# First layer of a two-layer decoder step: the row sums of the mixing weights, from four TensorE products with ones to one GpSimd sum over the partitions

## The chip, the cores and the metric

One core of a Trainium2 chip runs the whole step as one program. The metric is the device time of one execution in microseconds, the median over several runs. Beside it stands one execution that the hardware profiler recorded; its times count from its first instruction. The engines are TensorE (PE in the profile; its weight loads are PEld), VectorE (DVE), ScalarE (ACT), GpSimd (POOL) and SyncE (SP), which here issues all transfers.

## The reference

One inference step over 256 new prompt tokens and 8 x 8 sample tokens, all in float32. Layer 0 mixes tokens with a chunked spatial gating, layer 1 with a matrix memory; each layer ends with a gated MLP with a short convolution. The change touches only the mixer of layer 0:

```python
h = jax.nn.gelu(x @ w_in)
u, v = jnp.split(h, 2, axis=-1)
mu = jnp.mean(v, -1); var = jnp.mean(jnp.square(v - mu), -1)
v = (v - mu) * lax.rsqrt(var + EPS) * ln_g + ln_b
ws = jnp.where(mask, w_s[:, :L, :L], 0.0)          # 8 groups, L = 128
mixed = jnp.einsum('gts,bnsgd->bntgd', ws, vc) + b_s[:, :L].T[:, :, None]
y = (u * mixed.reshape(bsz, s, D_A)) @ w_out
```

`ln_b` is the same for every token s, so its part of the mixture is `ln_b` times the sum of `ws` over s. The kernel uses that: it mixes the normalised values without gain and shift, multiplies by the gain afterwards, and adds `ln_b` times these row sums. The row sums, one number for each of 8 groups and 128 target tokens, are what the change computes in another way.

## The kernel before

**Precision.** Weights and activations are float32. TensorE multiplies rounded halves: each operand is split into a rounded high half and the rest (`wh`, `wl` for weights, `xh`, `xl` for activations), and three products, high by high, high by low and low by high, are added in PSUM. For each chunk of weights, a tile of 128 partitions by up to 1024 elements, ScalarE casts the high half (L177) and VectorE subtracts it from the raw tile to get the low half (L178). The raw tiles have four buffers, the halves three; a buffer is taken again when TensorE has used the chunk three places before it.

**The order of the work in layer 0.** First come the values v, in natural layout (tokens on partitions), in four groups of 512 columns (`group(0)` to `group(3)`, products into `pv_a`); each group takes four chunks of 1024 columns. Between them lie the first norm (`rc`, made by GpSimd in L296), its spread over the partitions (`pb`), and, in `load_ws`, the transfers of the mixing weights `ws`, of a triangular mask `trit`, of the sample weights `wss` with their mask `bdt`, and of the biases `bs`. GpSimd then multiplies `ws` by the mask (L408) and both quarters of `wss` by theirs (L410). `v_out(q)` takes a group out of PSUM: gelu on ScalarE (L440), the joining of the sample parts (L435, L436) and statistics (L441).

After that come 16 blocks for u (`pm`, 24 products of 320 columns each). Behind block 0 stand `row_sums` and `v_stats`. `row_sums` splits the masked `ws` into two halves (`wsh` on ScalarE, `wsl` on VectorE, both L358), multiplies a matrix of ones by them (`pr`, two products for each half of the columns, so that every partition of the result holds the sums), and ScalarE copies the result into `rsum` (named `rs_a` in the profile, L421). `v_stats` joins the statistics and has GpSimd take the reciprocal root `rs` (`rstd_a`, L476); `normalise` (L482, ScalarE) applies it to the values. `mix(b)`, from block 4 on, multiplies the values by `ws` and `wss` (`pmix`), makes `b2` from `rsum`, `ln_b` and the biases (L519, VectorE), and then y (L522, L525, L528), which is split for the output projection.

**What sets the order.** TensorE's instructions, and most transfers, run in the order in which the program is written (`pin`). On ScalarE, VectorE and GpSimd a planner of the kernel language places each instruction in its engine's queue by modelled costs and by what it depends on; `issue_after` keeps an instruction behind another one. On the chip each engine then runs its queue in that fixed order, and waits where a semaphore has not been reached. The masking products L408 and L410 stand behind `rc`; the split of `ws` stands behind the latest weight split (`behind_split`).

Of the kernel before, what the change touches and what calls it, by code (L numbers as in the profile page):

```python
# [9 lines left out]

F32 = mybir.dt.float32
F32R = mybir.dt.float32r
# [4 lines left out]
P = 128  # L17
# [8 lines left out]
NH = 8  # L26
# [12 lines left out]
def halves(t):  # L39

    return t.rearrange("p (a b) -> p a b", a=2)


def parity(x):

    return x.rearrange("p (b a) -> p a b", a=2)
# [12 lines left out]
class Net:  # L59
# [301 lines left out]
    def layer_a(self):  # L361
        nc, tc, I, O = self.nc, self.tc, self.I, self.O
        with tc.tile_pool(name="ya", bufs=1) as yp, tc.tile_pool(name="la", bufs=1) as lp:
# [8 lines left out]
            ws = lp.tile([P, NH, P], F32, name="ws_a")  # L372
            wss = lp.tile([P, NH, P], F32, name="wss_a")
            bs = lp.tile([P, NH, P], F32, name="bs_a")
            rsum = lp.tile([P, NH, P], F32, name="rs_a")
# [21 lines left out]
            def load_ws():  # L397
# [9 lines left out]
                with tc.issue_after(self.rc_made.ins):  # L407
                    nc.gpsimd.tensor_tensor(ws, ws, trit.unsqueeze(1).to_broadcast([P, NH, P]), op=MULT)  # L408
                    for r, c in quads:
                        nc.gpsimd.tensor_tensor(wss[r, :, c], wss[r, :, c], bdt[r].unsqueeze(1).to_broadcast([64, NH, 64]), op=MULT)  # L410

            def row_sums():
                wsh = lp.tile([P, NH, P], F32R, name="wsh")
                wsl = lp.tile([P, NH, P], F32R, name="wsl")
                with self.behind_split():
                    self.split(wsh, wsl, ws)
                for i in range(2):
                    pr = self.psa.tile([P, 512], F32, tag="pa", name="pr")
                    for w, a, z in ((wsh, True, False), (wsl, False, True)):
                        self.mm(pr, self.onesr, w[:, 4 * i:4 * i + 4, :].rearrange("p g t -> p (g t)"), a, z)  # L420
                    nc.scalar.copy(rsum[:, 4 * i:4 * i + 4, :].rearrange("p g t -> p (g t)"), pr)  # L421

            def group(q, hooks, k=0):
                if q not in vps:
# [45 lines left out]
            def v_stats():  # L470
                for r, o in ((slice(64, P), slice(0, 64)), (slice(0, 64), slice(64, P))):
                    nc.scalar.copy(sts[r, 4:, :], sts[o, :4, :])
                for t in range(3):
                    nc.vector.bn_aggr(mv[:, t, :], st[:, t] if t < 2 else sts)
                nc.vector.tensor_scalar(ve, mv[:, :, 1], EPS, None, op0=ADD)
                nc.gpsimd.tensor_tensor(rs, ve, self.mhalf.to_broadcast([P, 3]), op=ALU.pow)  # L476
                nc.vector.scalar_tensor_tensor(ve, mv[:, :, 0], -1.0, rs, op0=MULT, op1=MULT)

            def normalise(q):
                for t in range(3):  # L480
                    vv = v[:, t, q * 512:(q + 1) * 512] if t < 2 else vs[:, 2 * q:2 * q + 2, :]
                    nc.scalar.activation(vv, vv, AF.Identity, scale=rs[:, t:t + 1], bias=ve[:, t:t + 1])  # L482
# [3 lines left out]
            def gains_in(q):  # L486
                cs = slice(q * 512, (q + 1) * 512)
                gB = lp.tile([P, 512], F32, tag="gB", name="gB", bufs=2)
                bB = lp.tile([P, 512], F32, tag="bB", name="bB", bufs=2)
                for par, r in enumerate((slice(64, P), slice(0, 64))):  # L490
                    self.pin(nc.sync.dma_start(gB[r], I["a_ln_g"][par:par + 1, cs].to_broadcast([64, 512])))
                    self.pin(nc.sync.dma_start(bB[r], I["a_ln_b"][par:par + 1, cs].to_broadcast([64, 512])))
                gains.append((gB, bB))
# [13 lines left out]
            def mix(b):  # L507
                g = b // 2
                pm = self.psa.tile([P, 512], F32, tag="pa", name="pmix")
                for t in range(2):  # L510
                    self.mm(pm[:, t * P:(t + 1) * P], v[:, t, b * P:(b + 1) * P], ws[:, g, :], True, True)
                if b % 2 == 0:

                    self.mm(pm[:, TP:TP + P], vs[:, g, :], wss[:, g, :], True, True)
                    ms[g] = pm[:, TP:TP + 64]
                    ms[g, 1] = pm[:, TP + 64:TP + P]
                sm = ms.pop((g, 1)) if b % 2 else ms.pop(g)
                b2 = lp.tile([P, 1, P], F32, tag="b2", name="b2", bufs=2)
                nc.vector.scalar_tensor_tensor(b2, rsum[:, g:g + 1, :], self.vec(V_LB + b), bs[:, g:g + 1, :], op0=MULT, op1=ADD)  # L519
                y = self.tp.tile([P, T], F32, tag="yf", name="y_a", bufs=2)  # L520
                lg = self.vec(V_LG + b)
                nc.vector.scalar_tensor_tensor(  # L522
                    y[:, :TP].rearrange("p (c t) -> p c t", c=2), pm[:, :TP].rearrange("p (c t) -> p c t", c=2), lg,
                    b2.to_broadcast([P, 2, P]), op0=MULT, op1=ADD)
                nc.vector.scalar_tensor_tensor(  # L525
                    y[:, TP:].rearrange("p (b t) -> p b t", b=NB), sm.rearrange("p (b t) -> p b t", b=NB), lg,
                    b2[:, :, :NS].to_broadcast([P, NB, NS]), op0=MULT, op1=ADD)
                nc.vector.tensor_tensor(y, y, us.pop(b), op=MULT)  # L528
                self.split_y(yh[:, b, :], yl[:, b, :], y)
# [4 lines left out]
            for b in range(16):  # L534
                ps = self.block(KD, self.x_rhs)
                if b == 0:
                    row_sums()
                    v_stats()
                t = lp.tile([P, T], F32, tag="ur", name="ur", bufs=2)
                nc.vector.tensor_tensor(halves(t), parity(ps[:, :T]), halves(self.rb), op=MULT)  # L540
                u = lp.tile([P, T], F32, tag="u", name="u", bufs=6)
                nc.scalar.activation(u, t, AF.Gelu_apprx_tanh)
                us[b] = u
                if 2 <= b < 2 + len(tables):
                    with tc.issue_after(self.last_load.ins):
                        nc.sync.dma_start(*tables[b - 2])
                if b in (9, 12):
                    gains_in(b // 3 - 3)
                if b in (0, 3, 6, 9):
                    normalise(b // 3)  # L550
                while mixed < min(b, b - 4 + max(0, b - 4) // 3 + 1):
                    mix(mixed)
                    mixed += 1
# [855 lines left out]
```

## Time and profile before

| | us |
|---|---|
| median of 3 runs | 882.37 |
| lowest, highest | 881.98, 882.60 |
| span of the profiled execution (first to last instruction) | 880.8 |
| TensorE busy in it | 874.7 (99%) |
| VectorE busy | 670.7 (76%) |
| ScalarE busy | 512.0 (58%) |
| GpSimd busy | 118.5 (13%) |

The profile gives no time of its own for the profiled execution beside the span; the median of the runs lies 1.6 us above it, which is what lies around the first and the last instruction.

A row of the timeline reads: start in us, duration in us (of all instructions merged in the row), engine, line, operation, output tile `<-` inputs, shapes, count, and in brackets the idle time before it with what ended it. A row of the view of one tile reads: line, engine, operation, tile, count, shortest / median / longest duration in ns, first and last start in us, forms. A row of DMA issues ends with the size of one and the us from issue to landing. The mean granted TensorE clock of the run was 0.999 of full speed.

### The profile page before, as it was taken

To read this page: it belongs to the slowest core of one execution; us is meant where nothing else is said; L and a number is where in the kernel's file an instruction comes from. 1 tells how busy PE (TensorE), PEld (TensorE's weight loads), DVE (VectorE), ACT (ScalarE), POOL (GpSimd) and SP (SyncE) were. 2 spreads that over 40 slices of the span, in tenths; PEclk is the share of its full clock that TensorE was granted. 3 is DMA by queue.
4 is the path that set the end of the run, shared out by engine and by line. 5 is a ranking of instruction groups with operands and counts; after the bars stand their busy time and mean duration, and the time that the engine had idled before them with its cause. 6 is when DMAs were issued, how large, how long until landed. Compare 5 with 4: busy or idle time off the path is not lost.

```text
span 880.8 us, 16999 instructions
## 1 busy us (share of the span) xinstructions
PE 874.7 (99%) x6424; PEld 857.2 (97%) x6424; DVE 670.7 (76%) x1291; ACT 512.0 (58%) x930; POOL 118.5 (13%) x288
## 2 busy tenths in 40 slices
PE   9999999999999999999999999999999999999997
PEld 7889999999999999999999999999999999999997
DVE  6866986578878865558999998878988788786443
ACT  6658554465555544347777775656766555554442
POOL 3200000020000000002433222303001000100000
PEclk9999999999999999999999999999999999999999
DMA  8755645545554455554847876665664544555551
GB/s 262 231 181 165 189 146 170 172 155 161 163 168 161 152 164 169 157 170 144 249 142 231 248 222 217 200 210 168 194 224 145 168 156 157 169 161 165 155 151 60
DMA packets 54950, 155.76 MB, mean 177 GB/s; under 512 B 7460, under 2 KB 12716, under 8 KB 54868
## 3 DMA queue, kind: packets, MB, share of 16 engines
q1 hardware_dynamic: 54868, 154.67, 55.9%
q8 instruction: 51, 0.84, 0.4%
q14 instruction: 31, 0.25, 0.1%
HBM read 142.66 MB, written 11.99 MB: 176 GB/s over the span
## 4 chain that ended last, share of the span: by engine, by line
PE 99%; DMA 0%; DVE 0%; ACT 0%; POOL 0%; issue 0%
PE pm L80 84%; PE pv_a L80 6%; PE num L80 2%; PE pmix L80 1%; PE pcs L80 1%; PE psc L80 1%; PE pCp L80 1%; PE phn L83 1%; PE pv L83 1%; PE pc L80 0%; DMA xT<-in_xv 0%; PE pk L83 0%; DVE y_p L687 0%; PE pg L80 0%; PE pb L80 0%; PE pr L80 0%
## 5 line engine op out<-in xcount | busy, mean ns | idle before, releaser
L178 DVE TENSOR_TENSOR wl<-raw,wh 128x1024 fp32r<-128x1024 f32 (+4 forms) x254 | 298.3, 1176 | 115.5 <-ACT wh L177 114.5
L177 ACT CAST wh<-raw 128x1024 fp32r<-128x1024 f32 (+4 forms) x254 | 255.5, 1007 | 215.5 <-PE pm L80 145.0
L80 PE MATMUL pm<-xh,wh 128*128 128x320 f32 x1216 | 356.6, 301 | 0.0
L80 PE MATMUL pm<-xl,wh 128*128 128x320 f32 x1216 | 354.7, 299 | 0.0
L80 PE MATMUL pm<-xh,wl 128*128 128x320 f32 x1216 | 308.9, 299 | 0.0
L80 PEld LDWEIGHTS pm<-xl,wh 128*128 128x128 f32 x1216 | 230.2, 189 | 0.1
L80 PEld LDWEIGHTS pm<-xh,wh 128*128 128x128 f32 x1216 | 230.1, 189 | 0.1
L80 PEld LDWEIGHTS pm<-xh,wl 128*128 128x128 f32 x1216 | 212.1, 189 | 0.0
L80 PE MATMUL pm<-yh_f,wh 128*128 128x320 f32 x352 | 105.3, 299 | 0.0
L80 PE MATMUL pm<-yh_f,wl 128*128 128x320 f32 x352 | 105.3, 299 | 0.0
L80 PE MATMUL pm<-yl_f,wh 128*128 128x320 f32 x352 | 105.3, 299 | 0.0
L80 PEld LDWEIGHTS pm<-yh_f,wl 128*128 128x128 f32 x352 | 66.6, 189 | 0.0
L80 PEld LDWEIGHTS pm<-yl_f,wh 128*128 128x128 f32 x352 | 66.6, 189 | 0.0
L80 PEld LDWEIGHTS pm<-yh_f,wh 128*128 128x128 f32 x352 | 66.6, 189 | 0.0
L593 DVE SCALAR_TENSOR_TENSOR fcv<-fpad,vecs,fcv 128x336 f32<-128x336 f32 x88 | 49.6, 566 | 2.1 <-ACT fcv L591 0.7
L595 ACT ACTIVATE fgl<-fcv 128x256 f32<-128x256 f32 x44 | 18.3, 416 | 37.3 <-DVE fcv L593 37.3
L80 PE MATMUL pm<-yh_a,wh 128*128 128x320 f32 x128 | 38.4, 300 | 0.0
L80 PE MATMUL pm<-yh_a,wl 128*128 128x320 f32 x128 | 38.3, 299 | 0.0
L80 PE MATMUL pm<-yl_a,wh 128*128 128x320 f32 x128 | 38.3, 299 | 0.0
L347 DVE TENSOR_TENSOR xT<-pm,xT 128x320 f32<-128x320 f32 x39 | 19.0, 486 | 24.4 <-PE pm L80 24.4
L80 PE MATMUL pm<-yhb,wh 128*128 128x320 f32 x128 | 35.9, 304 | 0.0
L80 PE MATMUL pm<-ylb,wh 128*128 128x320 f32 x128 | 35.5, 300 | 0.0
(273 smaller groups left out, 1263.8 us busy)
## 6 DMA issues: line engine op xcount, KB each, us to landing
raw<-in_f_up SPq DMA_DIRECT2D x88, 512.0 KB, 3.5
raw<-in_b_win SPq DMA_DIRECT2D x48, 512.0 KB, 4.5
raw<-in_f_dn SPq DMA_DIRECT2D x32, 448.0 KB, 3.3
C<-in_C SPq DMA_DIRECT2D x32, 258.0 KB, 4.9
out_Cs<-C SPq DMA_DIRECT2D x32, 258.0 KB, 4.8
raw<-in_a_win SPq DMA_DIRECT2D x16, 512.0 KB, 3.6
raw<-in_a_wo SPq DMA_DIRECT2D x16, 512.0 KB, 3.7
raw<-in_f_dn SPq DMA_DIRECT2D x16, 512.0 KB, 3.5
```

The lines of the kernel that those rows point to most:

```text
L80: self.pin(self.nc.tensor.matmul(out, lhsT, rhs, start=start, stop=stop, skip_group_check=skip))
L83: self.pin(self.nc.tensor.transpose(out, in_, ident))
L177: self.last_split = self.hold(nc.scalar.copy(wh[:, :kn, :], raw[:, :kn, :]))
L178: self.last_low = nc.vector.tensor_tensor(wl[:, :kn, :], raw[:, :kn, :], wh[:, :kn, :].bitcast(F32), op=SUB)
L347: self.nc.vector.tensor_tensor(x, ps[:, :T], x, op=ADD)
L593: nc.vector.scalar_tensor_tensor(cv, pd[:, i:i + NC], self.vec(w + i * KF), cv, op0=MULT, op1=ADD)
L595: nc.scalar.activation(gl[:, :TP], cv[:, :TP], AF.Gelu_apprx_tanh)
```

## The change

`row_sums` goes, with its call behind block 0: the split of `ws` into `wsh` and `wsl`, four products with ones, two copies out of PSUM. In its place `load_ws` gets one GpSimd instruction behind the masking products, which sums the masked `ws` (128 partitions x 1024 elements) over the partitions in float32 and writes the sums to all 128 partitions of `rsum`. The reader of `rsum`, L519, is unchanged.

```diff
+from concourse.bass_isa import ReduceOp
@@ load_ws, in tc.issue_after(self.rc_made.ins)
                     nc.gpsimd.tensor_tensor(ws, ws, trit.unsqueeze(1).to_broadcast([P, NH, P]), op=MULT)
                     for r, c in quads:
                         nc.gpsimd.tensor_tensor(wss[r, :, c], wss[r, :, c], bdt[r].unsqueeze(1).to_broadcast([64, NH, 64]), op=MULT)
-
-            def row_sums():
-                wsh = lp.tile([P, NH, P], F32R, name="wsh")
-                wsl = lp.tile([P, NH, P], F32R, name="wsl")
-                with self.behind_split():
-                    self.split(wsh, wsl, ws)
-                for i in range(2):
-                    pr = self.psa.tile([P, 512], F32, tag="pa", name="pr")
-                    for w, a, z in ((wsh, True, False), (wsl, False, True)):
-                        self.mm(pr, self.onesr, w[:, 4 * i:4 * i + 4, :].rearrange("p g t -> p (g t)"), a, z)
-                    nc.scalar.copy(rsum[:, 4 * i:4 * i + 4, :].rearrange("p g t -> p (g t)"), pr)
+                    nc.gpsimd.partition_all_reduce(rsum.rearrange("p g t -> p (g t)"), ws.rearrange("p g t -> p (g t)"), P, ReduceOp.add)
@@ the 16 blocks
             for b in range(16):
                 ps = self.block(KD, self.x_rhs)
                 if b == 0:
-                    row_sums()
                     v_stats()
```

## The prediction

> **What bounds the kernel now.** I read the page's busy times and chain first, then what is removed by its tiles, then TensorE in order of time around the four products.
>
> ```profile
> span 880.8 us, 16999 instructions
> PE 874.7 (99%) x6424; PEld 857.2 (97%) x6424; DVE 670.7 (76%) x1291; ACT 512.0 (58%) x930; POOL 118.5 (13%) x288
> PE 99%; DMA 0%; DVE 0%; ACT 0%; POOL 0%; issue 0%
> ```
>
> TensorE is busy for 874.7 of 880.8 us and 99% of the chain that ended last is TensorE's own order. So the time changes only by what is taken out of TensorE's order, or by what makes TensorE wait where it does not wait now. GpSimd is busy 13% and has room.
>
> ```profile
> L358 ACT CAST wsh<-ws_a x1: 1048/1048/1048, 58.9 to 58.9; 128x1024 fp32r<-128x1024 f32 x1
> L358 DVE TENSOR_TENSOR wsl<-ws_a,wsh x1: 1219/1219/1219, 60.2 to 60.2; 128x1024 fp32r<-128x1024 f32 x1
> L421 ACT COPY rs_a<-pr x2: 587/590/592, 66.8 to 67.3; 128x512 f32<-128x512 f32 x2
> ...
> 65.08 0.39 PE L80 MATMUL pr<-wsh,onesr 128*128 128x512 f32 x1
> ...
> 66.01 0.30 PE L80 MATMUL pm<-xh,wh 128*128 128x320 f32 x1
> ```
>
> The listed 0.39 us of one product overlaps the next. What the four occupy is from the start of the first, 65.08, to the start of the next block's first product, 66.01: 0.93 us.
>
> **What is removed.** From TensorE: 0.93 us, on the path. From ScalarE: one cast of ws (1.05 us) and two copies (0.59 us each). From VectorE: one subtraction of 1.22 us. These are worth nothing by themselves, because TensorE waited for neither engine there: the products of the blocks follow each other without a gap. The sum so far is -0.93 us.
>
> **What is added, and when it can start.** One GpSimd instruction over 128x1024, behind the three masking products and ahead of the reciprocal root L476 on the same in-order engine.
>
> ```profile
> 33.87 2.38 POOL L408 TENSOR_TENSOR ws_a<-ws_a,trit 128x1024 f32<-128x1024 f32 x1 [1.31 <-DMA trit<-in_trit]
> 36.34 2.70 POOL L410 TENSOR_TENSOR wss_a<-wss_a,bdt 64x512 f32<-64x512 f32 x2
> 69.17 0.85 POOL L476 TENSOR_TENSOR rstd_a<-ve_a,mhalf 128x3 f32<-128x3 f32 x1 [30.13 <-DVE ve_a L475]
> ```
>
> GpSimd is free from 39.04 (36.34 + 2.70) until 69.17, 30.1 us; that is the cover of the new instruction. It waits for nothing new, its input being done at 36.25.
>
> Its duration has no row. From below: one pass over 128x1024 elements, 2.38 us (L408). From above, if 128 partitions are halved seven times with a whole pass for each, 7 x 2.38 = 16.7 us. I take half of that, 8.3 us (an estimate): it has one input where L408 has two, and partial sums need not all be written back, but one pass cannot do it.
>
> None of the 288 GpSimd instructions of before is a sum over partitions, so its code may have to be brought in first, and the old code back afterwards. From below that costs 0. The nearest rows are ScalarE's table load and the landing of a 512 KB transfer in this very stretch.
>
> ```profile
> 0.81 1.28 ACT L1280 ACT_TABLE_LOAD   x1 [0.81 <-PEq L1389]
> ws_a<-in_a_ws SPq DMA_DIRECT2D x1, 512.0 KB, 5.5
> ```
>
> [...] Then the sum is ready to start at 39.04 + 5.5 = 44.5, ends about 8.3 us after it gets going, and a second 5.5 us for the way back still ends near 60, nine microseconds before L476 wants the engine. With a load of L and a sum of 8.3, L476 is on time while 2L + 8.3 stays under 30.1, that is L up to 10.9 us. [...]
>
> **What the new instruction collides with.** VectorE makes the low halves `wl` of the weights for every block, and reads two tiles from SBUF to do it. I looked at what VectorE and GpSimd do to each other where they overlap.
>
> ```profile
> 34.84 1.44 DVE L321 CAST rch<-rc 128x3 fp32r<-128x3 f32 x1
> 36.40 2.69 DVE L325 TENSOR_SCALAR dg<-ident,rch 128x128 fp32r<-128x128 f32 x3
> ...
> 421.65 1.10 DVE L358 TENSOR_TENSOR Pl<-Pf,Ph 128x384 fp32r<-128x384 f32 x1
> 421.31 1.04 POOL L977 TENSOR_TENSOR kgz<-kgs,mk 128x512 fp32r<-128x512 f32 x1 [0.71 <-DVE kgs L954]
> ...
> 435.82 0.85 POOL L1029 TENSOR_TENSOR sl<-t,mhalf 128x3 f32<-128x3 f32 x1 [3.07 <-DVE t L1027]
> 459.11 4.17 POOL L1029 TENSOR_TENSOR sl<-t,mhalf 128x3 f32<-128x3 f32 x1 [2.28 <-DVE t L1027]
> 458.95 1.22 DVE L178 TENSOR_TENSOR wl<-raw,wh 128x1024 fp32r<-128x1024 f32 x1
> 460.22 2.35 DVE L178 TENSOR_TENSOR wl<-raw,wh 128x1024 fp32r<-128x1024 f32 x2
> ```
>
> A cast of three columns takes 1.44 us and ends at 36.28, when L408 ends (36.25); the three `dg` of 36.40 end at 39.09, with L410 (39.04). `Pl` ends at 422.75, after `kgz` (422.35). The other way round, `sl`, 0.85 us at 435.82, takes 4.17 us while VectorE makes three `wl` back to back. So whichever of the two begins first keeps the other out to its end, and I let the whole 8.3 us block every two-input VectorE instruction behind it. [...]
>
> What is queued behind a blocked `wl` is the rest of VectorE's order, and TensorE waits for it. How late a `wl` may be is its first use by TensorE less 1.2 us for making it.
>
> ```profile
> 42.37 1.20 DVE L178 TENSOR_TENSOR wl<-raw,wh 128x1024 fp32r<-128x1024 f32 x1
> 43.97 2.36 DVE L178 TENSOR_TENSOR wl<-raw,wh 128x1024 fp32r<-128x1024 f32 x2
> 48.34 1.23 DVE L178 TENSOR_TENSOR wl<-raw,wh 128x1024 fp32r<-128x1024 f32 x1 [2.01 <-ACT wh L177]
> 52.71 1.23 DVE L178 TENSOR_TENSOR wl<-raw,wh 128x1024 fp32r<-128x1024 f32 x1 [0.51 <-ACT wh L177]
> 55.60 1.23 DVE L178 TENSOR_TENSOR wl<-raw,wh 128x1024 fp32r<-128x1024 f32 x1 [1.67 <-ACT wh L177]
> ...
> 44.26 0.59 PE L80 MATMUL pv_a<-wh,xh 128*128 128x512 f32 x2
> 45.33 0.59 PE L80 MATMUL pv_a<-wl,xh 128*128 128x512 f32 x2
> 54.91 0.60 PE L80 MATMUL pv_a<-wh,xh 128*128 128x512 f32 x2
> 55.99 0.59 PE L80 MATMUL pv_a<-wl,xh 128*128 128x512 f32 x2
> 59.44 0.59 PE L80 MATMUL pv_a<-wl,xh 128*128 128x512 f32 x2
> 62.09 0.30 PE L80 MATMUL pm<-xh,wl 128*128 128x320 f32 x1
> ...
> 47.26 1.05 ACT L177 CAST wh<-raw 128x1024 fp32r<-128x1024 f32 x1 [2.35 <-PE pv_a L80]
> ```
>
> The cast of 47.26 takes the buffer that the chunk begun at 44.26 has left; with three buffers it serves the third chunk after that one, begun at 54.91, whose first product with `wl` is at 55.99. Its `wl` (48.34) may therefore begin as late as 54.8. The one of 42.37 belongs to the chunk begun at 44.26 and is used at 45.33: it may begin no later than 44.1, 1.8 us after it does. By the same count of buffers the `wl` of 52.71 is first used at 59.44 and that of 55.60 at 62.09; these have 5.5 and 5.3 us to spare after their ends.
>
> With a start at 44.5, GpSimd finds VectorE in the two `wl` of 43.97, which end at 46.33. It runs from 46.33 to 54.6, the `wl` of 48.34 starts then, before 54.8, and TensorE does not wait. The next one (52.71) comes behind 2.6 us of other VectorE work (from 49.57 to 52.71, 0.51 of it idle): 54.6 + 1.2 + 2.6 = 58.4, where 58.2 is the latest, so at worst 0.2 us is lost of what is saved. From the ends: with 2.38 us nothing is felt at all; with 16.7 us the `wl` starts at 63.0, and TensorE waits 8.2 us.
>
> **The sum.** 880.8 - 0.93 = 879.9 us of span. The median of the runs is 882.37, 1.6 us above this span, which I keep: 881.4 us, 0.1% less. What can be told from no change here is 0.2%, 1.8 us; the change cannot save that much, so the forecast is no difference that can be measured.
>
> **The rivals.**
>
> Slower: the sum starts before the `wl` of 42.37. If its code costs little (the 1.28 us end), GpSimd is ready at 40.3, gets in there, and holds to 48.6. That `wl` should begin by 44.1, so TensorE waits 4.5 us; less 0.93 this is 885.9. It decides from a start before 42.37 and a duration over some 5.6 us. For it speaks that no load is seen in before; against it, that no such code runs in before either. 12%.
>
> Slower: L476 comes late, because the way back to the old code starts only when L476 is wanted, or because the loads are over 10.9 us.
>
> ```profile
> 70.25 1.52 ACT L482 ACTIVATE v_a<-v_a,ve_a,rstd_a 128x512 f32<-128x512 f32 x2 [1.42 <-DVE ve_a L477]
> 72.53 1.03 ACT L177 CAST wh<-raw 128x1024 fp32r<-128x1024 f32 x1
> 73.59 1.23 DVE L178 TENSOR_TENSOR wl<-raw,wh 128x1024 fp32r<-128x1024 f32 x1 [2.97 <-ACT wh L177]
> 76.06 0.30 PE L80 MATMUL pm<-xh,wl 128*128 128x320 f32 x1
> ```
>
> ScalarE already waits for L476 here, with the cast for a coming block queued behind; the `wl` made from it ends at 74.82 and is used at 76.06. There are 1.2 us to spare. A load of 5.5 us at that point makes 5.5 - 1.2 - 0.93, or 3.4 us: 885.8. Against it: nothing of a load has to wait for L476's input. 8%.
>
> Slower: the sum takes 16.7 us or more; 8.2 - 0.93 makes 889.6. If the partitions were added one after another at L408's price, 127 x 2.38 = 302 us, L476 would be ready some 277 us late and the time about 1158 us. 6%, most of it near the small end. [...]
>
> Slower: VectorE's order puts a reader of the sums (L519) earlier than they are there.
>
> ```profile
> 67.97 0.35 DVE L519 SCALAR_TENSOR_TENSOR b<-rs_a,vecs,bs_a 128x128 f32<-128x128 f32 x1
> 81.19 0.48 DVE L522 SCALAR_TENSOR_TENSOR y_a<-pmix,vecs,b 128x256 f32<-128x256 f32 x1
> ```
>
> Now it runs at 67.97, right after the copies, and its result is first used at 81.19. If it stands ahead of a `wl` and the sums come 8.3 us later than it, the 5.3 us to spare leave 3.0 us of waiting; less 0.93 this is 884.5. 5%.
>
> Faster by more: all later ScalarE and VectorE orders shift a little; TensorE's idle time outside the chain is at most 6.1 us, all but little at the two ends. With 2 us won it would be 880.4; 3%. That the change doesn't do what it says (products left in place) I hold at 1%: 882.4.
>
> **How the numbers follow.** The forecast, 881.4, has 65%; its own range is 881.0 to 884.5, where the upper end is a sum that catches the `wl` of 55.60 just before it begins (8.3 - 5.3 - 0.93 = 2.1 us). Up to 886.5 it takes in the first two rivals and the fourth; what stays out is the long sum and the little below 880.9. Range 880.9 to 886.5. Faster by over 0.2% (under 880.6): 4%. Slower by over 0.2% (over 884.1): 26%: the first three rivals, where they hold, and no more than the far edge of the forecast's own range and of the fourth. Within 0.2%: 70%.
>
> **What would show it.** In the changed profile: no `pr` products, and block after block at 65 us without a gap; a new GpSimd instruction between 39 and 69 us that starts near 46 and lasts near 8 us, or its start and length with the wait before it; a `wl` beside it that ends with it rather than after 1.23 us; L476 still near 69 and the cast behind L482 near 72. The prediction is wrong if TensorE shows idle time between 39 and 80 us, if the sum begins before 42 or lasts over 9 us and blocks VectorE, or if L476 starts late.

## The result and the profile after

| | before | after |
|---|---|---|
| median, 21 runs each, taken in turn (us) | 882.06 | 883.14 |
| lowest, highest | 881.93, 882.66 | 881.53, 884.74 |
| span of the profiled execution | 880.8 | 882.7 |
| time of the profiled execution | not given | 884.36 |

The ratio of after to before is 1.0013, with a 95% interval of 1.0007 to 1.0019. The change costs 1.1 us where 1.0 was to be won (882.37 to 881.4). That is within the 0.2% which the prediction counted as no difference, and inside its range, but the sign is the other one, and over these many runs the interval leaves out equality. The spread is the second difference: the runs of before lie within 0.7 us of each other, those of after within 3.2. The profiled execution of after is one of its slower ones, 1.2 us above the median; what its trace shows explains that execution first, and the spread is taken up with three more traces below.

The first three lines of the page of after, with the chain that ended last by engine:

```profile
span 882.7 us, 16992 instructions
PE 874.2 (99%) x6420; PEld 856.7 (97%) x6420; DVE 670.0 (76%) x1290; ACT 509.9 (58%) x927; POOL 126.0 (14%) x289
PE 87%; DVE 5%; DMA 3%; issue 1%; ACT 1%; POOL 1%; SPq 0%; DVEq 0%; POOLq 0%; ACTq 0%
```

TensorE has four products fewer and 0.5 us less to do, yet the span is 1.9 us longer. And the chain, which was 99% TensorE, now leaves it for 13% of the span: somewhere TensorE waits. The waits of TensorE in after (releaser, us in total, times, longest) name the places:

```profile
PE pv_a L81 <- DVE wl L179: 2.0, 1, 2.0
PE pw L81 <- PEq L1379: 0.8, 1, 0.8
PE pm L81 <- DVE yl_a L359: 0.5, 1, 0.5
```

The 0.8 us at the start stands in before too. The other two are new: 2.0 us for a low half of weights and 0.5 us for a split of y, -0.93 + 1.98 + 0.51 = +1.56 of the 1.9. The timelines of GpSimd, VectorE and TensorE in after, and below them TensorE in before at the same place, show how the longer one comes about:

```profile
34.70 2.37 POOL L409 TENSOR_TENSOR ws_a<-ws_a,trit 128x1024 f32<-128x1024 f32 x1 [2.57 <-DMA trit<-in_trit]
42.83 6.13 POOL L412 PARTITION_ALL_REDUCE rs_a<-ws_a  x1 [5.76 <-issue]
55.91 3.48 POOL L411 TENSOR_TENSOR wss_a<-wss_a,bdt 64x512 f32<-64x512 f32 x2 [6.95 <-DMA raw<-in_a_win]
70.49 0.90 POOL L467 TENSOR_TENSOR rstd_a<-ve_a,mhalf 128x3 f32<-128x3 f32 x1 [11.10 <-DVE ve_a L466]
```

```profile
40.80 1.21 DVE L179 TENSOR_TENSOR wl<-raw,wh 128x1024 fp32r<-128x1024 f32 x1
41.93 0.41 DVE L432 BATCH_NORM_STATS2 st_s<-v_s 128x6 f32<-128x256 f32 x1
49.00 0.61 DVE L510 SCALAR_TENSOR_TENSOR b<-rs_a,vecs,bs_a 128x128 f32<-128x128 f32 x2 [6.66 <-POOL rs_a L412]
49.53 3.49 DVE L179 TENSOR_TENSOR wl<-raw,wh 128x1024 fp32r<-128x1024 f32 x3
...
90.49 0.29 DVE L1282 TENSOR_TENSOR wg<-gate,xT 128x128 f32<-128x128 f32 x1 [1.77 <-DMA gate<-in_b_wg]
```

```profile
48.45 0.38 PE L81 MATMUL pv_a<-wh,xs_a 128*128 128x512 f32 x1
50.80 0.70 PE L81 MATMUL pv_a<-wl,xh 128*128 128x512 f32 x2 [1.98 <-DVE wl L179]
```

```profile
48.87 0.38 PE L80 MATMUL pv_a<-wh,xs_a 128*128 128x512 f32 x1
49.08 0.59 PE L80 MATMUL pv_a<-wl,xh 128*128 128x512 f32 x2
```

TensorE of after comes to this place 0.42 us earlier than that of before (48.45 and 48.87). Counted from start to start, as products overlap in the listing, the first wait costs 2.14 us (2.35 between the two rows of after, 0.21 in before) and the second, in the same way, 0.67 (0.81 and 0.14). With the four products this is -0.42 + 2.14 - 0.93 + 0.67 = 1.46 of the 1.9 us; the other 0.4 come in small steps later on, for which the record names no cause.

The planner did not leave the sum where the program has it. It put it ahead of the masking of `wss` (L411), and it put two readers of the sums (L510; it is the L519 of before, which first ran at 67.97) ahead of three `wl` in VectorE's queue. VectorE reaches these readers at 42.34 and stands still for 6.66 us until the sum has ended at 48.96. The first `wl` behind them ends at 50.76 (49.53 + 1.23), and TensorE wanted it at 48.82 (50.80 - 1.98). The chain of waits of after, in order of time (start, us, what), runs through just these pieces:

```profile
29.00 5.57 DMA trit<-in_trit
...
34.70 2.34 POOL ws_a L409
...
37.16 5.67 issue
42.83 6.14 POOL rs_a L412
...
49.53 1.23 DVE wl L179
...
50.80 1.35 PE pv_a L81 x5
```

So a transfer of a 64 KB mask, 5.7 us in which GpSimd does nothing that the trace names, and the sum itself have come onto the path.

The 0.5 us are further on: VectorE, in its fixed order, waits 1.77 us at `wg` for the weights of the gate (0.75 in before, at 88.10), and at 131.65 TensorE waits for the last of the splits of y. The same chain goes from the one to the other: from the gate's transfer, which starts at 85.87 and takes 4.59 us, almost only through VectorE's own order to the split of y that starts at 131.19 and to the product of 131.65.

### The profile page after: what moved, and what is told of

Same layout as the page of the kernel before. It is cut to its first block, busy times and chain, and to the rows that moved or that the text cites. A ratio compares the mean times of both kernels' runs of the same rounds, so it can differ in the third digit from the quotient of the medians.

```text
span 882.7 us, 16992 instructions
## 1 busy us (share of the span) xinstructions
PE 874.2 (99%) x6420; PEld 856.7 (97%) x6420; DVE 670.0 (76%) x1290; ACT 509.9 (58%) x927; POOL 126.0 (14%) x289
## 2 busy tenths in 40 slices
DMA packets 54950, 155.76 MB, mean 176 GB/s; under 512 B 7460, under 2 KB 12716, under 8 KB 54868
## 3 DMA queue, kind: packets, MB, share of 16 engines
q1 hardware_dynamic: 54868, 154.67, 55.6%
## 4 chain that ended last, share of the span: by engine, by line
PE 87%; DVE 5%; DMA 3%; issue 1%; ACT 1%; POOL 1%; SPq 0%; DVEq 0%; POOLq 0%; ACTq 0%
PE pm L81 79%; PE num L81 2%; DMA raw<-in_a_wv 2%; DVE wl L179 2%; PE pv_a L81 1%; PE pcs L81 1%; DVE yl_a L359 1%; POOL rs_a L412 1%; PE psc L81 1%; DVE y_a L519 1%; DMA trit<-in_trit 1%; PE pCp L81 1%; DVE y_a L513 1%; PE phn L84 1%; PE pv L84 1%
```

## The experiments

**The theory and its rival.** Theory A: the loss is the place of the readers in VectorE's queue, and only that; the sum itself is hidden. Theory B: the loss is what the sum does to VectorE while it runs, keeping its two-input instructions waiting, and would stay with the readers held back. The expectations name a theory C besides: loads of code, which no run shows, and the later changes of order cost it, whoever waits. A ratio is that to the kernel before, timed in the same comparison: 882.09 us (33 runs) for the first four kernels below, 882.15 (28 runs) for the four that follow; the three single executions at the end stand beside one of 882.38.

**Readers held behind the latest weight split, nothing else.**

```diff
-                nc.vector.scalar_tensor_tensor(b2, rsum[:, g:g + 1, :], ...)
+                with tc.issue_after(self.last_low.ins):
+                    nc.vector.scalar_tensor_tensor(b2, rsum[:, g:g + 1, :], ...)
```

> The changed kernel, with the readers of the sums (b2 on VectorE) held behind the latest low half of the weights, so that none of them can stand ahead of it in VectorE's queue. Theory A (VectorE's fixed queue: in the changed kernel two readers stand ahead of three low halves and wait 6.7 us for the sum): TensorE waits nowhere, VectorE has no wait for the sum, and the 0.93 us of the four products are won: 881.1 us against 882.1 before. Theory B (the sum itself keeps VectorE's two-input instructions out of SBUF): the low half beside the sum ends with the sum, after 4 to 6 us instead of 1.2; TensorE still waits up to 2 us if the sum gets in ahead of the first of the three: 881.1 to 883. Theory C (the code loads or later changes of order cost it): as the changed kernel, 883.1.

Measured: 882.25 us (881.21 to 882.63, 11 runs), 0.9 under after; the ratio to before is 0.9996 (0.9987 to 1.0005). TensorE's wait for `wl` is gone from its waits, the 0.5 us for the split of y stays. The time is 1.1 us above the 881.1 that theory A expected; the split of y accounts for half of that, the rest is open. The timelines of GpSimd, VectorE and TensorE in this kernel:

```profile
42.81 6.87 POOL L412 PARTITION_ALL_REDUCE rs_a<-ws_a  x1 [5.65 <-issue]
58.04 3.49 POOL L411 TENSOR_TENSOR wss_a<-wss_a,bdt 64x512 f32<-64x512 f32 x2 [8.36 <-issue]
```

```profile
42.47 1.22 DVE L179 TENSOR_TENSOR wl<-raw,wh 128x1024 fp32r<-128x1024 f32 x1
44.64 4.53 DVE L179 TENSOR_TENSOR wl<-raw,wh 128x1024 fp32r<-128x1024 f32 x1 [0.95 <-ACT wh L178]
...
88.42 0.29 DVE L1283 TENSOR_TENSOR wg<-gate,xT 128x128 f32<-128x128 f32 x1 [1.81 <-DMA gate<-in_b_wg]
```

```profile
52.25 0.59 PE L81 MATMUL pv_a<-wl,xh 128*128 128x512 f32 x2
```

The sum begins at the same time as in after (42.81, 42.83), so its start is not the difference. What B names is there: the `wl` of 44.64 takes 4.53 us instead of 1.2 and comes free 0.5 us before the sum ends (49.17 and 49.68), and the sum, which met the `wl` of 42.47 at its start, takes 6.87 us instead of 6.13. But the blocked `wl` is first used at 52.25, 3.1 us after its end. A holds for the 2.0 us; B is real and hidden.

**The sum added to the kernel before, its result unused; the products stay.**

```diff
+            spare = lp.tile([P, NH, P], F32, name="spare")
...
+                    nc.gpsimd.partition_all_reduce(spare..., ws..., P, ReduceOp.add)
```

> The kernel before with all its products, and the sum over the partitions beside it into a tile that nobody reads. [...] Theory A: as before, 882.1 us, no wait of TensorE. Theory B: low halves of the weights beside the sum last until its end; between 882.1 and 884, by what TensorE then waits. In both the sum lasts 6.1 us and GpSimd stands idle about 6 us ahead of it and again behind it.

Measured: 882.44 us (882.11 to 884.13, 11 runs), ratio 1.0006 (0.9997 to 1.0014). In its profile TensorE has only the 0.8 us wait of before, though the sum runs at 42.63 for 6.91 us and a `wl` takes 4.60 us beside it. The instruction by itself costs TensorE nothing in this execution. It is the fastest of the eleven (882.11), though, and three of the others lie at 883.2 to 884.1, which its trace does not explain.

**The change without the sum.** The other half alone; the sums are set to zero.

```diff
+            nc.gpsimd.memset(rsum, 0.0)
...
-                    nc.gpsimd.partition_all_reduce(rsum..., ws..., P, ReduceOp.add)
```

> The changed kernel without the sum: the row sums are left out, zeros set at the start stand in their place. What the four products are worth by themselves: the first product of block 1 follows block 0 at once, 0.93 us less than before, 881.1 us. If more than that is won or lost, the change of order on VectorE and ScalarE has a price of its own, which the changed kernel has too.

Measured: 881.64 us (881.15 to 882.73, 11 runs), ratio 0.9993 (0.9984 to 1.0002). The span of the profiled execution is 879.9, which is 0.9 under the 880.8 of before, as the removed products would have it; the median shows only half of it. The planner put the two readers early here too (43.22 in VectorE's order); with no sum to wait for they delay nothing, and TensorE has only the 0.8 us wait of before.

**Readers held, and the sum held behind both masks.** GpSimd then changes from masks to sum once, and the way back has until 68 us.

```diff
-                        nc.gpsimd.tensor_tensor(wss[r, :, c], ...)
+                        masked = nc.gpsimd.tensor_tensor(wss[r, :, c], ...)
+                with tc.issue_after(masked.ins):
                     nc.gpsimd.partition_all_reduce(rsum..., ws..., P, ReduceOp.add)
...
+                with tc.issue_after(self.last_low.ins):
+                    nc.vector.scalar_tensor_tensor(b2, rsum[:, g:g + 1, :], ...)
```

> As the first kernel of this set (readers held back), and the sum placed behind both products of wss with their mask, as the text of the change has it, where the planner had put it ahead of them. The sum then starts near 46 us, beside low halves that have 5 us and more to spare. Theories A and B: no wait of TensorE, 881.1 us; by B a low half that begins near 48 is drawn out to the sum's end near 52, and TensorE does not feel it.

Measured: 881.48 us (881.18 to 882.94, 11 runs), ratio 0.9992 (0.9983 to 1.0001), span 879.9. GpSimd in this kernel:

```profile
36.59 2.71 POOL L411 TENSOR_TENSOR wss_a<-wss_a,bdt 64x512 f32<-64x512 f32 x2
44.84 6.59 POOL L413 PARTITION_ALL_REDUCE rs_a<-ws_a  x1 [5.55 <-issue]
68.46 0.91 POOL L468 TENSOR_TENSOR rstd_a<-ve_a,mhalf 128x3 f32<-128x3 f32 x1 [17.03 <-DVE ve_a L467]
```

This is the order on GpSimd that the prediction had supposed, and the time that it gave (881.4); the readers stand even later than it had them, from 77.3 on. A `wl` beside the sum took 5.56 us, and no wait of TensorE came of it. `wg` waited 0.78 us for its transfer, and the 0.5 us gap is absent.

**The same order of GpSimd, but the readers where the planner puts them.**

```diff
                 with tc.issue_after(masked.ins):
                     nc.gpsimd.partition_all_reduce(rsum..., ws..., P, ReduceOp.add)
...
-                with tc.issue_after(self.last_low.ins):
-                    nc.vector.scalar_tensor_tensor(b2, rsum[:, g:g + 1, :], ...)
+                nc.vector.scalar_tensor_tensor(b2, rsum[:, g:g + 1, :], ...)
```

> The kernel with the sum behind the masking of wss (e4_sum_behind, 881.5), but with the readers left where the planner puts them: one low half later than in the changed kernel, still ahead of the next. Theory A: the sum ends near 51.4 us, the readers near 52.0, the low half behind them near 53.2, and TensorE, which wants it near 52, waits about 1 us: 882.3 us. Theory C: as e4_sum_behind, 881.5, since sum and loads are the same.

Measured: 883.5 us (881.73 to 885.37, 11 runs), ratio 1.0013 (1.0004 to 1.0022). Its waits and VectorE's readers:

```profile
PE pv_a L81 <- DVE wl L179: 2.3, 1, 2.3
...
PE pm L81 <- DVE yl_a L359: 0.5, 1, 0.5
```

```profile
52.62 0.61 DVE L511 SCALAR_TENSOR_TENSOR b<-rs_a,vecs,bs_a 128x128 f32<-128x128 f32 x2 [9.14 <-POOL rs_a L413]
```

Only the place of the readers differs from the kernel before this one in the list, and it costs 2.0 us, and the wide spread is back. Theory C, which expected 881.5, fails here: the sum (6.59 and 6.13 us) and the idle time ahead of it (5.55 and 5.52 us) are about the same. More was lost than expected: in the profiled execution (884.47) the sum ended at 52.58 (46.45 + 6.13) and not at 51.4, and TensorE waited 2.3 us where about 1 was expected. The place of the readers decides more than that of the sum: between the two kernels with the readers held, which differ in the place of the sum, lie 0.8 us, and their intervals overlap.

**The sum in two instructions of four groups each,** with the readers left early: if they wait for the first half only, the wait should shrink.

```diff
-                    nc.gpsimd.partition_all_reduce(rsum..., ws..., P, ReduceOp.add)
+                    for g in (0, 4):
+                        nc.gpsimd.partition_all_reduce(rsum[:, g:g + 4, :]..., ws[:, g:g + 4, :]..., P, ReduceOp.add)
```

> The changed kernel with the sum made in two instructions of four groups each. VectorE's queue stays as in the changed kernel, with two readers ahead of three low halves; these two readers need only the first half. Theory A (the place of the readers in VectorE's queue and what they wait for set TensorE's wait): VectorE waits some 3 us less than 6.7, which is more than the 2.0 us that TensorE waited for the low half; that wait goes, and the time is 881.1 to 881.7. Theory C (code loads and changes of order cost it, whoever waits): as the changed kernel, about 883. [...]

Measured: 887.72 us (886.32 to 889.55, 6 runs; the slowest is the profiled one), ratio 1.006 (1.0048 to 1.0072). The first wait did go: the readers stood still for 3.51 us instead of 6.66, and TensorE no longer waits at 48.8. But the planner put the masks between the halves. GpSimd and the waits of TensorE in this kernel:

```profile
42.72 3.25 POOL L413 PARTITION_ALL_REDUCE rs_a<-ws_a  x1 [5.83 <-issue]
53.53 4.32 POOL L411 TENSOR_TENSOR wss_a<-wss_a,bdt 64x512 f32<-64x512 f32 x2 [7.56 <-DMA raw<-in_a_win]
63.97 3.25 POOL L413 PARTITION_ALL_REDUCE rs_a<-ws_a  x1 [6.12 <-issue]
74.95 0.90 POOL L468 TENSOR_TENSOR rstd_a<-ve_a,mhalf 128x3 f32<-128x3 f32 x1 [7.72 <-issue]
```

```profile
PE pm L81 <- ACT wh L178: 4.5, 1, 4.5
...
PE pm L81 <- DVE wl L179: 0.4, 1, 0.4
```

Each change between masks or roots and the sum has some 6 to 8 us of idle GpSimd ahead of it (5.83, 7.56, 6.12 and 7.72 us), and there are four changes. The last comes ahead of the reciprocal root, 5.8 us later than the 69.17 of before, and the cast queued behind it on ScalarE is late for TensorE: the prediction's second rival, with its own term (5.8 less the 1.2 us to spare is 4.6; 4.5 were measured). The products then run on at half the granted clock up to 84.8, which costs another 2.7 us (the last section has the rows): -0.93 + 4.5 + 0.4 + 2.7 = 6.7 of the 6.9 us by which the span of 887.7 exceeds the 880.8 of before. Theory A's number for the whole, 881.1 to 881.7 us, was missed: it reckons with no price for the added changes.

**The gate's weights multiplied later,** behind the last weight split of the layer, once on top of the held readers and sum, and once on the kernel before.

```diff
-            nc.vector.tensor_tensor(self.wg[:, :, :16], raw, ...)
-            nc.scalar.copy(self.gsum, self.gate[:, P:])
+            with self.behind_split():
+                nc.vector.tensor_tensor(self.wg[:, :, :16], raw, ...)
+                nc.scalar.copy(self.gsum, self.gate[:, P:])
```

> The kernel with the sum behind the masking of wss and the readers held back (e4_sum_behind), and besides the two small instructions that wait for the transfer of the gate weights (wg on VectorE, gsum on ScalarE) moved from the middle of layer 0 to its end. They waited 0.8 to 1.8 us for that transfer, and in the two traces with 1.8 us TensorE waited 0.5 us for the last low half of y at 129 to 131 us. If that wait is what makes single runs of one kernel differ by 0.6 us, the runs now lie together: 881.2 us, none over 882; the 0.93 us of the four products are won in full against 882.1.

> The kernel before with the same move of wg and gsum alone. If the wait for the gate weights is what spreads its runs between 881.9 and 882.8, they lie together at 882.0; its time hardly changes. Against e5_gate_late the difference should be the 0.9 us of the four products.

Measured: on the held kernel 881.37 us (881.13 to 881.72, 11 runs), ratio to before 0.9991 (0.9983 to 1.0000), no wait of TensorE but the 0.8 at the start; on the kernel before 882.19 us (881.95 to 882.64, 11 runs), ratio 1.0 (0.9992 to 1.0009). So the gate's transfer is not what spreads the runs of before, which was a miss; on the held kernel the runs do lie closer together than without the move (881.18 to 882.94), but there one run alone lies above 881.9. The two kernels with the same move differ by 0.82 us, which agrees with the 0.93 us of products and leaves little that is lost on the way. The first of them is the fastest kernel of the study: 0.8 us under before, with an interval that just touches equality, and by the medians 1.8 us under after.

**The changed kernel three more times, unedited,** to see what its spread is made of.

> The changed kernel once more, unchanged, for a second trace of it. Its runs lay between 881.5 and 884.7 us, those of before between 881.9 and 882.7. [...]

> As a1: a further trace of the changed kernel. Theory A: TensorE's wait at the low half is 1.98 us plus or minus what the sum ends later or earlier than 48.96, measured against TensorE's own position. Another theory (TensorE's clock, or waits elsewhere, make the spread): no such relation, and waits at other places.

> As a1 and a2: a third further trace of the changed kernel, with the same expectation. The time should be about 881.1 us plus this wait, plus up to 0.5 us where the wait for the gate weights near 88 us is 1.8 us.

| execution | time | mask done by | sum ends | VectorE stands still | TensorE waits for `wl` | for the split of y |
|---|---|---|---|---|---|---|
| first | 882.45 | 34.89 | 46.74 | 6.25 | 0 | 0.5 |
| second | 881.83 | 34.95 | 47.21 | 6.58 | 0 | 0 |
| profiled after | 884.36 | 37.07 | 48.96 | 6.66 | 1.98 | 0.5 |
| third | 885.59 | 37.34 | 49.20 | 7.02 | 2.3 | 0 |

GpSimd in the first and in the third:

```profile
32.51 2.38 POOL L409 TENSOR_TENSOR ws_a<-ws_a,trit 128x1024 f32<-128x1024 f32 x1
40.61 6.13 POOL L412 PARTITION_ALL_REDUCE rs_a<-ws_a  x1 [5.72 <-issue]
```

```profile
34.97 2.37 POOL L409 TENSOR_TENSOR ws_a<-ws_a,trit 128x1024 f32<-128x1024 f32 x1 [2.93 <-DMA trit<-in_trit]
43.07 6.13 POOL L412 PARTITION_ALL_REDUCE rs_a<-ws_a  x1 [5.73 <-issue]
```

In the first two executions the mask `trit` is there when GpSimd comes to it; in the other two GpSimd waits 2.6 to 2.9 us for it. These 2 us pass straight into the end of the sum and from there to TensorE, whose wait for `wl` follows the end of the sum as theory A expected. In before the same wait (1.31 us) was of no consequence, since nothing near it read the result. Where the mask lands early, TensorE does not wait for `wl`: 881.83 us, and 882.45 with the gap for the split of y, beside 881.4 forecast and 882.38 for the one execution of before. The times themselves were expected lower, at 881.1 us and the waits: the first two and the profiled one lie 0.7 to 0.9 above that, which is open, and the third 2.2, most of which the last section explains.

## Why the prediction was right or wrong

**The products, 0.93 us: right.** The profiled spans without TensorE's new waits are 879.9 (no sum), 879.9 and 879.7 (both held), against 880.8, and the pair with the gate moved differs by 0.82 us. The medians of these kernels show 0.4 to 0.8 us against before, less than the spans.

**The time ahead of the sum, 5.5 us: right on the way there, short on the way back.** 5.5 to 6.1 us of idle GpSimd stand ahead of the sum in every kernel that has it; 6.95 to 8.4 us stand between the sum and what comes straight behind it. No run shows that this is a load of code, as the prediction supposed: the trace puts this time down to "issue" or, in some rows, to a transfer, and the page of after counts exactly as many packets in each queue as that of before (54868, 51 and 31). So no run shows the term of 5.5 us as a load; in its place the runs showed idle time of these lengths, and its cause is open.

**The duration, 8.3 us: mis-sized,** it is 6.13 us, and 6.6 to 6.9 where it meets a running `wl`. Two halves take 3.25 us each, so here it grew with the columns (2.88 us for 512 more, 5.6 ns each).

**The collision with VectorE: right.** The `wl` beside the sum takes 4.53, 4.60, 5.56 and 4.53 us instead of 1.2 and ends 0.5 us before it, and TensorE does not feel it, in four kernels of four where the readers were out of the way.

**The start of the sum, behind the masks of `wss` at 46.33: wrong.** It was taken from the order of the program; the planner put the sum ahead of those masks, and it started between 40.6 and 43.1. Whether that alone helps or costs is not shown: with the readers held, the kernel with the early sum took 882.25 us and the one with the sum behind the masks 881.48.

**The step that failed** is in the fourth rival: "Now it runs at 67.97, right after the copies". The forecast let the reader stay there, with the rest of VectorE's order as in before, and held 5% against it. But the reader stood at 67.97 only because the products made the sums then. With sums that come earlier, the planner moved the first two readers up with them, to the place that VectorE reaches at 42.34, ahead of three `wl`; by what cost it chose that place the record does not show. The rival's mechanism is what happened. Its price was 3.0 us from a sum of 8.3 less 5.3 us to spare; with the measured wait of 6.66 us, 0.53 us for the two readers and 5.25 us to spare (from 42.34, where VectorE was free for the `wl`, to 47.59, its latest start for a use at 48.82), it is 6.66 + 0.53 - 5.25 = 1.94; measured 1.98. Less the 0.93 us of products the profiled run would lose 1.05 us; the second wait, 0.51, had not been foreseen at all.

**The other rivals.** The late root did not happen in after (L467 still waits for its input at 70.49), but splitting the sum brought it about at its predicted price. The first rival did not happen: the sum did begin before 42.37 in two executions (40.61 and 41.08), but the `wl` in question had ended ahead of it (38.96 + 1.23 = 40.19 in the first). Nor did a sum of 16.7 us or more. The chances hold a slip: the 884.5 of the fourth rival lies above the 884.1 from which "slower by over 0.2%" counts, yet its 5% stand with the 70% of no difference.

**What stays open.** Why the mask lands early in some executions and late in others (it was issued at 26.8 and 27.1 and took 5.0 and 5.2 us where it was early; it was issued at 29.0 and took 5.6 us in the profiled after, and was issued at 26.7 and took 8.1 us in the third execution); why `wg` waits 0.8 to 1.2 us in some and 1.8 in others (in all the profiles with `wg` in its old place the 0.5 us gap followed where it waited 1.77 us or more, and did not where it waited 1.18 or less; the chain of after joins the two, but no run moves `wg` alone in after); and the three longer executions of the kernel with the unused sum.

## What to carry to other kernels

Where a planner orders the engines, a producer that is moved forward takes its readers along: look where they land in an in-order queue, and hold them behind the work that the critical engine wants next, since an engine off the path costs nothing only as long as nothing critical is queued behind a reader of its result (here the unused sum made TensorE wait for nothing, the one with readers ahead of three `wl` for 1.98 us). Keep instructions of one kind together on GpSimd when another kind is brought in, for GpSimd stood idle for 5.5 to 8.4 us at each change of kind here where the next instruction was ready. And a wait that was of no consequence (a mask landing 2 us late) becomes spread in the time as soon as its result is wanted early.

## What had not been expected of the hardware

In two runs a pause of TensorE cost more than itself. In the third unedited execution it lasted 2.31 us (48.73 to 51.04); the windows that follow (us, then busy time of PE, PEld, DVE, ACT and POOL, the granted clock, DMA share, GB/s):

```profile
50.00:52.00 2.00, 0.96 (x3) 0.84 (x4) 2.00 (x2) 0.00 (x0) 0.00 (x0) 0.85 0.02 6
52.00:54.00 2.00, 2.00 (x6) 1.53 (x6) 1.94 (x4) 0.25 (x1) 0.00 (x0) 0.50 0.91 295
54.00:56.00 2.00, 2.00 (x9) 1.68 (x8) 1.86 (x4) 1.20 (x3) 0.00 (x0) 0.80 0.94 289
```

The granted clock was 0.85 in the first of these windows, 0.50 in the next and 0.80 in the third, where six and nine products ran in the last two: 2 x 0.15 + 2 x 0.5 + 2 x 0.2 = 1.7 us lost beside the pause. If the clock was either full or 0.50 within them, it was 0.50 from 51.4 to 54.8, for 3.4 us (an estimate from these three windows). Counted from start to start the pause cost 2.5 us, and TensorE had come to it 0.6 us earlier than in the second execution: 2.5 + 1.7 - 0.6 = 3.6 of the 3.7 us by which its span (883.8) exceeds that one's (880.1). After pauses of 1.98 us (profiled after) and 2.3 us (readers early behind both masks) the granted clock was 1.00 in every window from 40 to 100 us; in the kernel with the sum in two halves the pause of 4.5 us ended at 79.43, and by the same estimate the granted clock was 0.50 from 78.0 (it was 1.00 from 74 to 78) to 84.8, for 6.8 us, so that the products from 79.4 on lost half of 5.4 us, 2.7. The same view:

```profile
80.00:82.00 2.00, 1.64 (x7) 1.32 (x6) 1.03 (x2) 2.00 (x5) 0.00 (x0) 0.50 0.26 20
82.00:84.00 2.00, 2.00 (x9) 2.00 (x8) 1.39 (x2) 2.00 (x4) 0.00 (x0) 0.50 0.71 283
84.00:86.00 2.00, 2.00 (x13) 2.00 (x13) 1.27 (x2) 2.00 (x5) 0.00 (x0) 0.80 0.59 147
```

So the length of a pause does not decide by itself: the one of 2.31 us in the third execution was followed by a lower clock, the one of 2.29 us with the readers early behind both masks (52.13 to 54.42) was not. What decides it, and why the clock was low for 3.4 us in the one run and for 6.8 us in the other, no run here shows.
